# mLSTM sums over v from rounded halves, two gate rows through DRAM, and first outputs split behind the delta rule

## The chip, the cores and the metric

The kernel runs on one core of one Trainium2 chip. The metric is the device time of one execution, in microseconds (us). The core has five engines with an instruction queue each: TensorE (PE: matmuls and transposes, PEld: its weight loads), VectorE (DVE), ScalarE (ACT), GpSimd (POOL) and SyncE (SP, which here only issues DMAs). GpSimd computes little in this kernel; it issues the DMAs that are not of SP. All DMAs share 16 DMA engines.

## The reference

One layer of a hybrid encoder block in fp32, for 256 tokens of 2048 channels. The parts that matter here:

```
mod = silu(c) @ W_ada + b_ada     -> shift, scale, gate of the mixer; shift, scale, gate of the FFN
h   = RMSNorm(x) * (1 + scale_m) + shift_m
p   = h @ W_in                    -> inputs of the mLSTM (a), of the delta rule (b), merge gates
A   = bidirectional mLSTM         (4 heads, keys of 256, values of 512)
B   = bidirectional gated delta rule  (16 heads of 128)
y   = sigmoid(g_a) * (A @ W_a) + sigmoid(g_b) * (B @ W_b)
x   = x + gate_m * (y @ W_o)
x   = x + gate_f * SwiGLU(RMSNorm(x) * (1 + scale_f) + shift_f)      (width 5632)
```

and a last RMSNorm. For one head and one direction the mLSTM is a decayed attention, `h_t = sum_s P[t,s] v_s / max(|sum_s P[t,s]|, ...)`, where `P` is the product of query and key times the gates' decay.

## The kernel before

**Rounded halves.** The weights are fp32. The kernel splits each operand in two: a half `h` rounded to the format fp32r (a copy by ScalarE) and the remainder `l` (a subtraction by VectorE), and makes a product from three fp32r passes: `xh*wh`, `xl*wh`, `xh*wl`. `split(hi, lo, v)` does that for an operand that lies on the chip. `tjob` (L169) does it for a projection with two blocks of 128 tokens and 512 output columns: it loads the weights in chunks of 1.05 MB (`raw`, three buffers, issued on SP), splits each chunk as two halves of 128x1024 (`wh`, `wl`, three buffers each) and issues 12 passes of 512 columns for each half into two accumulators (`acc`). A chunk's `raw` buffer is free again when both its halves are split.

**Products that are not split.** A few products are made in plain fp32. Those of this change are the mLSTM's sums over `v` (`ph`, L977), whose operands are the decayed scores `dec` (tile `mdec`) and the values `vt`, and four products for each gate row.

**The order of the work.** The Python code is a set of generators that are advanced in turn (`fill`, `drive`, `steps`); a scheduler then orders each engine's instructions when the program is built, by priorities that follow that order and by its own estimates. `order(...)` keeps an instruction at its place in the order of the code. What comes out is a fixed order for each engine and each DMA queue: an instruction whose operand isn't there holds up all that stand behind it.

**The stretch around the change**, in the order of the code:

- The delta rule for its last four heads ends. Its outputs go through DRAM (`ob_d`) and come back as `o4_0` to `o4_3` (`o_load`, on GpSimd's queue). `o_split` makes of each a quarter of `obh` and `obl`, the operand of the projection `yb`.
- The loop of three: `fill(2)` issues the last products of the input projection (among them `ma3`, whose read-out is `ev_ma3` at L317), then `o_split(g)`.
- `y_b(g)`, g from 0 to 3, projects the delta rule's outputs with the weights `wbb`, four chunks for each g (`yb0_0` to `yb0_3`). Between its halves stand the steps of the four mLSTM heads, two at a time: `mlstm(h)` loads `mkq` (keys and queries), `vt`, `sgo` (the output gate) and `bc` (the decays) on GpSimd's queue; VectorE makes `mdec` by scans; TensorE makes the scores `psc`, then the denominators `pden`, then the sums `ph`; ScalarE reads out `dn` and `hs`. The result, normalised and times the gate, is transposed (`pxa`) into `hah` and `hal`.
- `y_a(g)` projects these with `wba`, merges both branches in `mg` and transposes that to `mgh` and `mgl`. Then comes the output projection `o0` to `o3`, whose `residual` reads `gm`, the mixer's gate as a row on all partitions.
- The FFN: gate and up projection (`gt`, `up`), down projection `d`, whose `residual` reads the other gate row, `gf`.

**The gate vectors.** `mod` holds the modulation with channels on partitions: 16 columns for each of its six parts. `ada_part` (L115) makes part 2 and the following ones in the background: for each column one load of 1.05 MB on SP (tile `ada`) and one multiply-and-sum on VectorE; `pump` advances them between the weight halves and `sums()` directly. `row(part, dst, ...)` (L1080) turns one part into a row on all partitions: for each quarter VectorE makes four scaled diagonals (`dg`), TensorE multiplies them by a matrix of ones, ScalarE copies the product to `dst`. It stands for `gm` behind the load of `x1`, ahead of the output projection, and for `gf` ahead of the down projection.

Of the kernel before, what the change touches and what calls it, by code (L numbers as in the profile page):

```python
# [9 lines left out]
F32 = mybir.dt.float32  # L10
# [5 lines left out]
P = 128  # L16
T = 256
D = 2048
# [34 lines left out]
def hybrid_block(ctx: ExitStack, tc: tile.TileContext, xr, nfr, crow, pk_d, cst_d, ada2, ada4, win0, winb, wint, wba, wbb, wo, wgu, wd, out, dbg=None):  # L53
# [31 lines left out]
    def order(ins, yes=True):  # L85

        return tc.keep_in_program_order(ins) if yes else ins
# [43 lines left out]

    background = []
# [36 lines left out]
    def tjob(name, chunks, xh, xl, done, early=0, by_token=None, steps=1):  # L169
# [6 lines left out]
        def halves(u, k0):  # L176
            if u not in raws:
                raws[u] = st.tile([P, 4, 512], F32, tag="raw", bufs=3, name=f"raw_{name}_{u}")
                nc.sync.dma_start(raws[u], chunks[u])
            wh = st.tile([P, 2, 512], F32R, tag="wh", bufs=3, name=f"wh_{name}_{u}_{k0}")  # L180
            wl = st.tile([P, 2, 512], F32R, tag="wl", bufs=3, name=f"wl_{name}_{u}_{k0}")
            order(S.activation(wh, raws[u][:, k0 : k0 + 2], AF.Copy), early)  # L182
            order(V.tensor_tensor(wl, raws[u][:, k0 : k0 + 2], wh.bitcast(F32), ALU.subtract), early)  # L183
            return wh, wl
# [45 lines left out]
    def run(job):  # L230
        for _ in job:
            pass
# [682 lines left out]
    def mlstm(h):  # L915
# [19 lines left out]
        for t in range(2):  # L935
# [17 lines left out]
            (0, 0): [(dec[:, 0, 0:P], 0)],  # L953
            (0, 1): [(dec[:, 0, P:256], 0), (dec[:, 0, 256:384], 1)],
            (1, 0): [(dec[:, 1, 256:384], 0), (dec[:, 1, 0:P], 1)],
            (1, 1): [(dec[:, 1, P:256], 1)],
        }
        pd_ = gps(f"pden{h}")
        for (d, t), terms in src.items():
            for i, (w, s) in enumerate(terms):  # L960
                PE.matmul(pd_[:, 2 * t + d : 2 * t + d + 1], w, ones1, start=i == 0, stop=i == len(terms) - 1)
# [8 lines left out]
        yield  # L970
        for t in range(2):
            pn = []
            for d in range(2):
                ph = gps(f"ph{h}_{t}_{d}")
                terms = src[d, t]
                for i, (w, s) in enumerate(terms):
                    PE.matmul(ph, w, vt[:, s], start=i == 0, stop=i == len(terms) - 1)  # L977
                pn.append(ph)
            S.activation(hs[:, t], pn[0], AF.Copy, scale=dn[:, t, 0:1])
            V.scalar_tensor_tensor(hs[:, t], pn[1], dn[:, t, 1:2], hs[:, t], ALU.mult, ALU.add)  # L980
            S.activation(sq, hs[:, t], AF.Square, accum_out=ss[:, t : t + 1])
            yield
# [19 lines left out]
    def y_b(g):  # L1002
# [6 lines left out]
        return tjob(f"yb{g}", [wbb[g, u] for u in range(4)], obh, obl, done)  # L1009
# [30 lines left out]
    for g in range(3):  # L1040
        fill(2)
        o_split(g, o4s[g])
# [10 lines left out]
    mg = mgp.tile([P, 2, D], F32, name="mg")  # L1053

# [8 lines left out]
    for g in range(4):  # L1063
        if g == 3:
            every[0] = 0
        run(y_a(g, mgh, mgl))
    while len(background) > 2:
        sums()
# [11 lines left out]
    def row(part, dst, rp, factor=1.0):  # L1080

        for g in range(4):
            dg = rp.tile([P, 4, P], F32, tag="dg", bufs=2, name=f"dg{part}_{g}")
            for e in range(4):
                c = part * KB + 4 * g + e
                V.tensor_scalar(dg[:, e], ident, mod[:, c : c + 1], factor, ALU.mult, ALU.mult)
            pr = gps(f"row{part}_{g}")
            PE.matmul(pr, ones, dg.rearrange("p e c -> p (e c)"), start=True, stop=True)
            S.activation(dst[:, g * 512 : (g + 1) * 512], pr, AF.Copy)

    gm = wp.tile([P, D], F32, name="gm")
    row(2, gm, wp, 0.5)
# [149 lines left out]
    row(5, gf, dp)  # L1242
# [134 lines left out]
```

## Time and profile before

| | us |
|---|---|
| timed, median of three | 1998.9 (1995.4 to 2001.5) |
| the profiled execution | 1998.51 |
| its span | 1996.5 |
| mean granted TensorE clock | 0.990 of full |

The span is the time from the first to the last instruction that the profile shows; the 2.0 us beside it lie around it. `L123` is line 123 of the kernel. A group is written `out<-in partitions x elements`, an engine's name ahead of the operation. `idle before` is the time that the engine stood still just ahead of those instructions, with the instruction or DMA that ended most of it.

### The profile page before, as it was taken

How to read it: one execution, taken by the hardware profiler on the slowest of the kernel's cores; microseconds unless marked ns; L12 is line 12 of the kernel's file. 1: busy time of each engine (PE TensorE's matmuls, PEld its weight loads, DVE VectorE, ACT ScalarE, POOL GpSimd, SP SyncE). 2: the span in 40 equal slices, each digit the busy share in tenths (PEclk: the TensorE clock that was granted, in tenths of full speed). 3: DMA queues.
4: the chain of work that ended last, by engine and by line, in shares of the span. 5: the costliest groups of instructions: out<-in, count | busy, mean ns of one | idle time of the engine just before them, and what ended most of it. 6: DMA issues, size and time to landing. Idle time of an engine off the chain costs nothing.

```text
span 1996.5 us, 26938 instructions
## 1 busy us (share of the span) xinstructions
PE 1935.0 (97%) x10310; PEld 1697.5 (85%) x10310; DVE 1392.7 (70%) x2099; ACT 1020.6 (51%) x1558; POOL 94.7 (5%) x181
## 2 busy tenths in 40 slices
PE   8998999999999889999899999899999999999997
PEld 6887889988989888989777888688888888888886
DVE  5777987778988787865677779765666665555554
ACT  3145757754774566555453444554444444444443
POOL 0001200110100010100100000000000000000000
PEclk9998999999999999999999999999999999999999
DMA  9986674567676665876787679457676675555553
GB/s 400 420 355 193 197 231 169 177 200 256 209 237 222 212 197 208 284 284 238 298 313 259 241 279 413 166 218 261 235 267 237 232 268 199 208 205 198 209 200 138
DMA packets 78322, 485.64 MB, mean 243 GB/s; under 512 B 10201, under 2 KB 15585, under 8 KB 23793
## 3 DMA queue, kind: packets, MB, share of 16 engines
q1 hardware_dynamic: 63360, 450.95, 62.2%
q0 software_dynamic: 7520, 17.88, 4.3%
q10 hardware_dynamic: 7314, 15.10, 2.0%
q8 instruction: 81, 1.33, 0.3%
q14 instruction: 47, 0.39, 0.1%
HBM read 467.07 MB, written 16.82 MB: 242 GB/s over the span
## 4 chain that ended last, share of the span: by engine, by line
PE 78%; DMA 9%; DVE 7%; ACT 4%; issue 2%; ACTq 0%; POOL 0%; SPq 0%; DVEq 0%; POOLq 0%
PE acc_up L200 4%; PE acc_up L203 4%; PE acc_up L201 4%; PE acc_d L203 4%; PE acc_d L201 4%; PE acc_d L200 4%; PE acc_gt L201 4%; PE acc_gt L200 4%; PE acc_gt L203 4%; DMA ra<-ada 3%; PE acc_b L161 3%; PE acc_o L203 2%; PE acc_o L200 2%; PE acc_o L201 2%; PE acc_a L161 2%; DMA raw_b<-winb 2%
## 5 line engine op out<-in xcount | busy, mean ns | idle before, releaser
L183 DVE TENSOR_TENSOR wl_d<-raw_d,wh_d 128x1024 fp32r<-128x1024 f32 x88 | 107.7, 1224 | 102.3 <-ACT wh_d L182 100.3
L183 DVE TENSOR_TENSOR wl_up<-raw_up,wh_up 128x1024 fp32r<-128x1024 f32 x88 | 107.7, 1225 | 101.2 <-ACT wh_up L182 101.2
L126 DVE SCALAR_TENSOR_TENSOR ada<-ada,crow 128x2048 f32<-128x2048 f32 x64 | 146.4, 2288 | 41.9 <-DMA ada<-ada 41.8
L182 ACT ACTIVATE wh_d<-raw_d 128x1024 fp32r<-128x1024 f32 x88 | 93.0, 1057 | 128.5 <-PE acc_d L201 122.8
L182 ACT ACTIVATE wh_gt<-raw_gt 128x1024 fp32r<-128x1024 f32 x88 | 92.9, 1056 | 120.7 <-PE acc_gt L201 73.2
L182 ACT ACTIVATE wh_up<-raw_up 128x1024 fp32r<-128x1024 f32 x88 | 93.0, 1057 | 120.5 <-PE acc_up L201 72.9
L183 DVE TENSOR_TENSOR wl_gt<-raw_gt,wh_gt 128x1024 fp32r<-128x1024 f32 x88 | 107.1, 1223 | 68.1 <-ACT wh_gt L182 47.3
L161 PE MATMUL acc_b<-hh,wh_b 128*128 128x256 f32 x576 | 140.8, 285 | 7.7 <-ACT wh_b L157 7.7
L161 PE MATMUL acc_b<-hl,wh_b 128*128 128x256 f32 x576 | 141.2, 286 | 0.0
L200 PE MATMUL acc_gt<-wh_gt,hfh 128*128 128x512 f32 x352 | 135.7, 385 | 0.1
L201 PE MATMUL acc_gt<-wh_gt,hfl 128*128 128x512 f32 x352 | 135.0, 384 | 0.0
L200 PE MATMUL acc_up<-wh_up,hfh 128*128 128x512 f32 x352 | 133.4, 379 | 0.0
L201 PE MATMUL acc_up<-wh_up,hfl 128*128 128x512 f32 x352 | 133.4, 379 | 0.0
L200 PE MATMUL acc_d<-wh_d,ffh 128*128 128x512 f32 x344 | 130.8, 380 | 0.0
L201 PE MATMUL acc_d<-wh_d,ffl 128*128 128x512 f32 x344 | 130.8, 380 | 0.0
L515 PE MATMUL first<-x,raw 128*128 128x256 f32 x512 | 114.5, 382 | 7.6 <-ACT x L508 7.6
L161 PEld LDWEIGHTS acc_b<-hh,wh_b 128*128 128x128 f32 x576 | 112.7, 196 | 9.9 <-ACT wh_b L157 8.3
L515 PEld LDWEIGHTS first<-x,raw 128*128 128x128 f32 x512 | 96.0, 190 | 26.1 <-ACT x L508 13.6
L161 PEld LDWEIGHTS acc_b<-hl,wh_b 128*128 128x128 f32 x576 | 112.9, 196 | 2.3 <-issue 2.2
L158 DVE TENSOR_TENSOR wl_b<-raw_b,wh_b 128x1024 fp32r<-128x1024 f32 x72 | 87.4, 1219 | 32.1 <-ACT wh_b L157 31.5
L157 ACT ACTIVATE wh_b<-raw_b 128x1024 fp32r<-128x1024 f32 x72 | 75.1, 1055 | 58.2 <-DMA raw_b<-winb 31.0
L182 ACT ACTIVATE wh_o<-raw_o 128x1024 fp32r<-128x1024 f32 x64 | 67.2, 1056 | 64.7 <-PE acc_o L201 27.2
(370 smaller groups left out, 4990.8 us busy)
## 6 DMA issues: line engine op xcount, KB each, us to landing
ada<-ada SPq DMA_DIRECT2D x64, 1024.0 KB, 5.2
raw_gt<-wgu SPq DMA_DIRECT2D x44, 1024.0 KB, 5.3
raw_up<-wgu SPq DMA_DIRECT2D x44, 1024.0 KB, 5.0
raw_d<-wd SPq DMA_DIRECT2D x44, 1024.0 KB, 4.9
raw_b<-winb SPq DMA_DIRECT2D x36, 1024.0 KB, 5.9
ra<-ada SPq DMA_DIRECT2D x32, 1025.0 KB, 15.7
raw<-win SPq DMA_DIRECT2D x16, 1024.0 KB, 14.5
raw_z<-wint SPq DMA_DIRECT2D x16, 1024.0 KB, 5.6
```

Of the source, the lines that this page charges most:

```text
L126: V.scalar_tensor_tensor(raw, raw, 1.0, row_c[:, :D], ALU.mult, ALU.mult, accum_out=mod[:, c0 + b : c0 + b + 1])
L157: S.activation(wh, raw[:, k0 : k0 + 8], AF.Copy)
L158: V.tensor_tensor(wl, raw[:, k0 : k0 + 8], wh.bitcast(F32), ALU.subtract)
L161: PE.matmul(o, wh[:, k], both(x, k0 + k).rearrange("p a b -> p b a"), start=k0 + k + i == 0, stop=False)
L182: order(S.activation(wh, raws[u][:, k0 : k0 + 2], AF.Copy), early)
L183: order(V.tensor_tensor(wl, raws[u][:, k0 : k0 + 2], wh.bitcast(F32), ALU.subtract), early)
L200: order(PE.matmul(ps[t], tok(xh, kk, t), turns(wh[:, k]), start=kk == 0, stop=False), early and steps > 1)
L201: PE.matmul(ps[t], tok(xl, kk, t), turns(wh[:, k]), start=False, stop=False)
L203: PE.matmul(ps[t], tok(xh, kk, t), turns(wl[:, k]), start=False, stop=kk == last)
L515: PE.matmul(first[o], raw[:, o], x[:, b], start=b == 0 and o % 2 == 0, stop=b == KB - 1 and o % 2 == 1)
```

## The change

There are three parts, which meet in the stretch described above.

1. *The sums over v* are made from rounded halves like the projections: `dec` is split to `dch` and `dcl`, `vt` to `vth` and `vtl`, and each of a head's six fp32 products becomes three fp32r passes. `vth` lies in the buffer of `o4_3`; the others lie in a new pool, `mp`. The generator stops once behind both blocks of tokens where it stopped behind each.
2. *The gate rows* are made by one transpose of the part's 16 columns (16 rows of 128), a copy on ScalarE, a store of the 2048 values to DRAM (`row_store`) and a load that puts them on all partitions (`row_load`), both on GpSimd's queue. For `gm` the store is called ahead of the last quarter of `ya`, and with it the loop over the leftover `sums()`; the load is called where `row` was. For `gf` both are called where `row` was.
3. *The outputs of the delta rule*: in the loop of three, `o_split(g)` is called ahead of `fill(2)`. And for the second chunk of `yb0` (halves 2 and 3, `held`) the two splits are kept at their place in the order of the code.

```diff
+    def row_store(part, rp, factor=1.0):
+        pr = gps(f"row{part}")
+        PE.transpose(pr[0:KB, 0:P], mod[:, part * KB : (part + 1) * KB], ident)
+        sm = rp.tile([KB, P], F32, name=f"rowsm{part}")
+        S.activation(sm, pr[0:KB, 0:P], AF.Copy, scale=factor)
+        G.dma_start(row_d[part].rearrange("(b p) -> b p", b=KB), sm)
+
+    def row_load(part, dst):
+        G.dma_start(dst, row_d[part].partition_broadcast(P))
...
-            order(S.activation(wh, raws[u][:, k0 : k0 + 2], AF.Copy), early)
-            order(V.tensor_tensor(wl, raws[u][:, k0 : k0 + 2], wh.bitcast(F32), ALU.subtract), early)
+            hold = early or 2 * u + k0 // 2 in held
+            order(S.activation(wh, raws[u][:, k0 : k0 + 2], AF.Copy), hold)
+            order(V.tensor_tensor(wl, raws[u][:, k0 : k0 + 2], wh.bitcast(F32), ALU.subtract), hold)
...
+        dch, dcl = (mp.tile([P, 2, 384], F32R, name=f"d{n}{h}", tag=f"d{n}", bufs=1) for n in ("ch", "cl"))
+        vth = ml.tile([P, 2, DV_A], F32R, tag="o4", bufs=1, name=f"vth{h}")
+        vtl = mp.tile([P, 2, DV_A], F32R, tag="vtl", bufs=1, name=f"vtl{h}")
+        split(dch, dcl, dec)
+        split(vth, vtl, vt)
         for t in range(2):
             pn = []
             for d in range(2):
                 ph = gps(f"ph{h}_{t}_{d}")
-                terms = src[d, t]
-                for i, (w, s) in enumerate(terms):
-                    PE.matmul(ph, w, vt[:, s], start=i == 0, stop=i == len(terms) - 1)
+                terms = [(x, y, *q) for x, y in ((dch, vth), (dcl, vth), (dch, vtl)) for q in src[d, t]]
+                for i, (x, y, c, s) in enumerate(terms):
+                    PE.matmul(ph, x[:, d, c : c + P], y[:, s], start=i == 0, stop=i == len(terms) - 1)
...
-            yield
+        yield
...
-        return tjob(f"yb{g}", [wbb[g, u] for u in range(4)], obh, obl, done)
+        return tjob(f"yb{g}", [wbb[g, u] for u in range(4)], obh, obl, done, held=() if g else (2, 3))
...
     for g in range(3):
+        o_split(g, o4s[g])
         fill(2)
-        o_split(g, o4s[g])
...
         if g == 3:
             every[0] = 0
+            while len(background) > 2:
+                sums()
+            row_store(2, ml, 0.5)
         run(y_a(g, mgh, mgl))
-    while len(background) > 2:
-        sums()
...
-    row(2, gm, wp, 0.5)
+    row_load(2, gm)
...
-    row(5, gf, dp)
+    row_store(5, dp)
+    row_load(5, gf)
```

How the built programs differ is seen at three places. The first is ScalarE's queue behind the delta rule. The first number behind a tile's name is its group, head or chunk (`wh_yb0_1_0` is the first half of `yb0`'s second chunk), the last only numbers the tile. Before:

```order
L182 ACTIVATE wh_yb0_0_2_9250<-raw_yb0_0_9232 128x1024
L182 ACTIVATE wh_yb0_1_0_9303<-raw_yb0_1_9301 128x1024
L317 ACT_TABLE_LOAD
L317 ACTIVATE ev_ma3_9208<-acc_ma3_0_9042 128x512
L317 ACTIVATE ev_ma3_9208<-acc_ma3_1_9043 128x512
L318 DMA ma_d3_109<-ev_ma3_9208 128x1024
L912 ACTIVATE obh_8828<-o4_0_8084 128x1024
L912 ACTIVATE obh_8828<-o4_1_8086 128x1024
L912 ACTIVATE obh_8828<-o4_2_8443 128x1024
```

And of the change, from the second quarter of `obh` on:

```order
L926 ACTIVATE obh_8830<-o4_1_8088 128x1024
L926 ACTIVATE obh_8830<-o4_2_8445 128x1024
L926 ACTIVATE obh_8830<-o4_3_8832 128x1024
L259 ACTIVATE vth0_9379<-vt0_8836 128x1024
L1004 ACTIVATE sgo0_8838<-sgo0_8838 128x1024
L259 ACTIVATE dch0_9377<-mdec0_9114 128x768
L1004 ACTIVATE sgo1_8847<-sgo1_8847 128x1024
L977 ACTIVATE dn0_9283<-pden0_9276 128x4
L998 ACTIVATE hs0_9288<-ph0_0_0_9385,dn0_9283 128x512
L977 ACTIVATE dn1_9298<-pden1_9291 128x4
L196 ACTIVATE wh_yb0_1_0_9308<-raw_yb0_1_9306 128x1024
```

The first split of `yb0`'s second chunk stood ahead of `ev_ma3` and of all of `obh`; it now stands behind all four quarters of `obh` and behind ScalarE's part of head 0 up to the first read-out of its sums.

The second place is TensorE's queue between the first and the third chunk of `yb0`. Before, where the scores of head 0 stood between two chunks:

```order
L203 MATMUL acc_yb0_0_9230<-wl_yb0_1_2_9320,obh_8828 128x512
L203 MATMUL acc_yb0_1_9231<-wl_yb0_1_2_9320,obh_8828 128x512
L203 MATMUL acc_yb0_0_9230<-wl_yb0_1_2_9320,obh_8828 128x512
L203 MATMUL acc_yb0_1_9231<-wl_yb0_1_2_9320,obh_8828 128x512
L937 MATMUL psc0_9117<-mkq0_8832 128x256 x4
L200 MATMUL acc_yb0_0_9230<-wh_yb0_2_0_9337,obh_8828 128x512
```

And of the change, behind the first chunk:

```order
L217 MATMUL acc_yb0_1_9236<-wl_yb0_0_2_9256,obh_8830 128x512
L951 MATMUL psc0_9119<-mkq0_8834 128x256 x4
L951 MATMUL psc1_9133<-mkq1_8843 128x256 x4
L975 MATMUL pden0_9276<-ones_81,mdec0_9114 128x1 x6
L975 MATMUL pden1_9291<-ones_81,mdec1_9128 128x1 x2
L996 MATMUL ph0_0_0_9385<-vth0_9379,dch0_9377 128x512
L996 MATMUL ph0_0_0_9385<-vth0_9379,dcl0_9378 128x512
L996 MATMUL ph0_0_0_9385<-vtl0_9380,dch0_9377 128x512
...
L996 MATMUL ph0_1_1_9406<-vtl0_9380,dch0_9377 128x512
L214 MATMUL acc_yb0_0_9235<-wh_yb0_1_0_9308,obh_8830 128x512
```

The scores of heads 0 and 1, denominators of both and all 18 passes of head 0's sums now stand between the first and the second chunk of `yb0`; before, the second chunk came first, only head 0's scores stood ahead of the third, and the rest came later.

The third place is the end of GpSimd's queue, behind the loads of heads 2 and 3. Before, nothing followed there:

```order
L924 DMA bc3_9761<-mal_d_93 128x256 x2
L919 DMA vt2_9748<-v_d2_100 128x1024
L919 DMA vt3_9757<-v_d3_101 128x1024
L921 DMA sgo2_9750<-o_d2_104 128x1024
L921 DMA sgo3_9759<-o_d3_105 128x1024
L1372 UNCONDITIONAL_BRANCH
```

And of the change:

```order
L935 DMA sgo2_9724<-o_d2_106 128x1024
L935 DMA sgo3_9733<-o_d3_107 128x1024
L140 DMA row_d2_89<-rowsm2_10663 16x128
L143 DMA gm_10837<-row_d2_89 128x2048
L140 DMA row_d5_90<-rowsm5_14920 16x128
L143 DMA gf_14915<-row_d5_90 128x2048
L1383 UNCONDITIONAL_BRANCH
```

Four DMAs are added there, a store and a load for each row.

More of the change, by code (lines that the diff above doesn't have):

```diff
@@ L129, in ada_part @@
         yield True
+    row_d = {part: tc.dram_tile([D], F32, name=f"row_d{part}") for part in (2, 5)}
+    def row_store(part, rp, factor=1.0):
[6 more added lines that the diff above has]
+        G.dma_start(dst, row_d[part].partition_broadcast(P))
     background = []
@@ L167, in fjob, with tjob @@
             yield True
-    def tjob(name, chunks, xh, xl, done, early=0, by_token=None, steps=1):
+    def tjob(name, chunks, xh, xl, done, early=0, by_token=None, steps=1, held=()):
         raws = {}
@@ L952, in mlstm @@
         src = {
[L953 to L956, printed above, removed]
+            (0, 0): [(0, 0)],
+            (0, 1): [(P, 0), (256, 1)],
+            (1, 0): [(256, 0), (0, 1)],
+            (1, 1): [(P, 1)],
         }
@@ L959, in mlstm @@
         for (d, t), terms in src.items():
-            for i, (w, s) in enumerate(terms):
-                PE.matmul(pd_[:, 2 * t + d : 2 * t + d + 1], w, ones1, start=i == 0, stop=i == len(terms) - 1)
+            for i, (c, s) in enumerate(terms):
+                PE.matmul(pd_[:, 2 * t + d : 2 * t + d + 1], dec[:, d, c : c + P], ones1, start=i == 0, stop=i == len(terms) - 1)
         dn = ml.tile([P, 2, 2], F32, tag="dn", bufs=2, name=f"dn{h}")
@@ L974, in mlstm @@
                 ph = gps(f"ph{h}_{t}_{d}")
-                terms = src[d, t]
-                for i, (w, s) in enumerate(terms):
-                    PE.matmul(ph, w, vt[:, s], start=i == 0, stop=i == len(terms) - 1)
+                terms = [(x, y, *q) for x, y in ((dch, vth), (dcl, vth), (dch, vtl)) for q in src[d, t]]
+                for i, (x, y, c, s) in enumerate(terms):
+                    PE.matmul(ph, x[:, d, c : c + P], y[:, s], start=i == 0, stop=i == len(terms) - 1)
                 pn.append(ph)
@@ L1053, in hybrid_block @@
     mg = mgp.tile([P, 2, D], F32, name="mg")
+    mp = pool(sd, "mp", side="right")
     every[0] = 2
@@ L1078, in hybrid_block @@
     S.dma_start(x1, xr)
[L1080 to L1089, printed above, removed]
     gm = wp.tile([P, D], F32, name="gm")
-    row(2, gm, wp, 0.5)
+    row_load(2, gm)
     def residual(t, g, ps, gate, ss, rp, hold=False):
```

## Prediction

> **What bounds the kernel now.** I read the page's busy times and chain first, then who TensorE waits for, then the stretch around the delta rule's end in five-microsecond windows, and last that stretch engine by engine in the timeline.
>
> ```profile
> span 1996.5 us, 26938 instructions
> PE 1935.0 (97%) x10310; PEld 1697.5 (85%) x10310; DVE 1392.7 (70%) x2099; ACT 1020.6 (51%) x1558; POOL 94.7 (5%) x181
> PE 78%; DMA 9%; DVE 7%; ACT 4%; issue 2%; ACTq 0%; POOL 0%; SPq 0%; DVEq 0%; POOLq 0%
> ```
>
> TensorE is busy for 97% of the span and is 78% of the chain. So a pass taken off TensorE is worth its length, and work put on VectorE or ScalarE is free as long as TensorE isn't made to wait for it. Who it waits for from the delta rule's end to the FFN:
>
> ```profile
> PE pxn L1184 <- ACT xn L1177: 8.4, 7, 3.4
> PE acc_yb L200 <- DMA ada<-ada: 6.0, 1, 6.0
> PE acc_o L203 <- DVE wl_o L183: 0.8, 2, 0.6
> ```
>
> The first row belongs to the norm ahead of the FFN, which the change leaves alone. The second is the place of this change: one wait of 6.0 us. In windows (PE busy, granted clock, DMA share, GB/s):
>
> ```profile
> 965.00:970.00 5.00, 4.07 (x19) 1.00 0.85 278
> 970.00:975.00 5.00, 0.00 (x0) 0.78 1.00 422
> 975.00:980.00 5.00, 4.86 (x11) 0.54 1.02 366
> ...
> 990.00:995.00 5.00, 5.00 (x25) 1.00 1.01 404
> 995.00:1000.00 5.00, 5.00 (x31) 1.00 1.04 386
> ```
>
> After the wait TensorE runs on half its clock for most of 975 to 980, which costs (1 - 0.54) x 5 = 2.3 us more; from 980 on it has no gap, while the DMA engines are full at 0.40 MB/us. ScalarE's, TensorE's and GpSimd's rows say why it waited:
>
> ```profile
> 969.91 1.06 ACT L182 ACTIVATE wh_yb<-raw_yb 128x1024 fp32r<-128x1024 f32 x1 [3.21 <-DMA raw_yb<-wbb]
> 970.98 1.28 ACT L317 ACT_TABLE_LOAD   x1
> 974.00 2.95 ACT L912 ACTIVATE obh<-o 128x1024 fp32r<-128x1024 f32 x3 [0.63 <-ACT ev_ma L317]
> ...
> 975.10 1.22 PE L200 MATMUL acc_yb<-wh_yb,obh 128*128 128x512 f32 x2 [6.04 <-DMA ada<-ada]
> ...
> 971.47 0.81 POOL L866 DMA_DIRECT2D o<-ob_d  x1 [123.51 <-ACT wh_yb L182]
> 985.12 0.54 POOL L924 DMA_DIRECT2D bc<-mal_d  x1 [0.73 <-DMA vt<-v_d]
> ```
>
> `obh`, which the first product of `yb0` reads, stood in ScalarE's line behind a split that waited for its weights. The mLSTM's loads for heads 0 and 1 go out on GpSimd's queue from 971.5 to 985.
>
> **The change, part by part.** *The sums over v.* A head had 6 fp32 products; it now has 18 of rounded halves.
>
> ```profile
> L977 PE MATMUL ph<-vt,mdec 128*128 128x512 f32 x48 | 22.0, 594 | 0.0
> 1192.03 0.86 PE row L1088 x2
> 1195.47 0.86 PE acc_o L203 x4
> ```
>
> 24 products are 48 passes, so an fp32 product is two; by the chain two such passes take 0.86 us and four passes of rounded halves the same 0.86, so 0.43 and 0.215 each. A head goes from 6 x 0.86 = 5.2 us to 18 x 0.215 = 3.9: **-1.3 us a head**, -3.9 for heads 1 to 3; head 0 is counted below with its surroundings. For each head the splits add an operation over 128x1024 and one over 128x768 to VectorE and to ScalarE:
>
> ```profile
> L183 DVE TENSOR_TENSOR wl_yb<-raw_yb,wh_yb 128x1024 fp32r<-128x1024 f32 x31 | 37.2, 1220 | 10.0 <-ACT wh_yb L182 9.9
> 980.00:1110.00 130.00, 129.88 (x591) 104.89 (x590) 98.35 (x142) 61.80 (x91) 7.39 (x13) 1.00 0.79 292
> ```
>
> On VectorE that is 4 x (1.22 + 0.92) = 8.6 us, the 768 columns scaled from 1024; ScalarE's two are shorter. VectorE is busy 98 of the 130 us of this stage (third figure) and ScalarE 62, so 107 of 130 still fits and I take nothing. Without that cover it would be those 8.6 us.
>
> *The gate rows.* Each row drops four fp32 products (4 x 0.86 = 3.45 us), 16 small VectorE products and four copies, and adds one transpose of 128 columns (0.22 us, a quarter of an 0.86), one copy and two DMAs on GpSimd. For `gf` nothing is near: its first reader is a whole group of the down projection later, 22 weight halves, some 57 us at the 2.59 us a half shown below. **-3.2 us.** `gm` loads 1.05 MB in the stage of the output projection:
>
> ```profile
> 1186.00:1250.00 64.00, 64.00 (x293) 54.35 (x292) 58.61 (x72) 29.30 (x37) 0.00 (x0) 1.00 1.01 416
> 1203.58 1.07 ACT L182 ACTIVATE wh_o<-raw_o 128x1024 fp32r<-128x1024 f32 x1 [1.44 <-DMA raw_o<-wo]
> 1208.25 0.38 PE L200 MATMUL acc_o<-wh_o,mgh 128*128 128x512 f32 x1
> ```
>
> The DMA engines have no room there for 64 us. The first weights of group 1 came in at 1203.6 and were split by 1204.65, 3.6 us before TensorE took them at 1208.25. With 1.05 / 0.416 = 2.5 us of transfer more ahead of them, TensorE can come at most 3.6 - 2.5 = 1.1 us earlier. Ends: -3.2 (the load slips in behind) and -1.1; by the row above I take **-1.1**. The Trainium skill's page "DMA: Bandwidth & Descriptors", section "Issuing engines are not separate DMA queues", says that transfers issued from different engines run on the same 16 DMA engines and interleave. By it GpSimd's queue buys this load no bandwidth, which is the -1.1; were the queue a path of its own, the sum would be 2.1 us lower. The trace's 1.01 agrees.
>
> The loop over the leftover sums moves ahead of the last quarter of `ya`. VectorE's order of sums is the same up to there, so it issues nothing at either place.
>
> *The place.* ScalarE's order now has all four `obh`, then `vth0`, `sgo0`, `dch0`, `sgo1`, `dn0`, `hs0`, `dn1`, and only then the second weights of `yb0`. `obh` no longer waits for weights, which saves the first 3 us of the old wait. But TensorE's order, too, has both heads' scores and all of head 0's sums between the first and second weights of `yb0`, where six halves of `yb0` ran before. Everything now stands behind head 0's chain, and that behind loads:
>
> ```profile
> 988.35 1.06 ACT L985 ACTIVATE sgo<-sgo 128x1024 f32<-128x1024 f32 x1 [2.56 <-DMA sgo<-o_d]
> 998.43 1.06 ACT L985 ACTIVATE sgo<-sgo 128x1024 f32<-128x1024 f32 x1 [3.15 <-DMA sgo<-o_d]
> ...
> 998.81 0.69 DVE L928 TENSOR_TENSOR_SCAN mdec<-bc,cst 128x256 f32<-128x256 f32 x1 [2.27 <-DMA bc<-mal_d]
> 1000.72 0.46 DVE L946 SCALAR_TENSOR_TENSOR mdec<-psc,eT,mdec 128x256 f32<-128x256 f32 x1
> ...
> 979.68 2.76 SPq L179 DMA_DIRECT2D raw_yb<-wbb  x2
> 987.08 0.33 SPq L125 DMA_DIRECT2D ada<-ada  x1
> ```
>
> The last load, head 1's `bc`, landed at 998.8, since three 1.05 MB loads of SP's ran beside GpSimd's in full DMA windows. Two of them (the second at 979.68 and the one at 987.08) need buffers that only the held splits set free, so they come later now: 2.1 / 0.40 = 5.2 us, and `bc` lands at **993.6**. Ends: 990.9 (all three out of the way, 7.9 us) and 998.8 (none). From there head 1's scans and first score product take 998.81 to 1001.18, so 2.4 us: TensorE gets its next row at 996.0. Then head 0's sums 3.9, six small rows 0.6 (half of the twelve below), and, as TensorE has idled again, the slow clock's 2.3 (ends 0 and 4.5): `yb0` goes on at **1002.8**. ScalarE's split for it is issued behind `dn1`, two thirds through the sums, and hides.
>
> Where was TensorE at 1002.8 before?
>
> ```profile
> 1000.55 0.38 PE L200 MATMUL acc_yb<-wh_yb,obh 128*128 128x512 f32 x1
> ...
> 1003.14 0.38 PE L200 MATMUL acc_yb<-wh_yb,obh 128*128 128x512 f32 x1
> ...
> 1003.79 1.40 PE L961 MATMUL pden<-ones,mdec 128*128 128x1 f32 x12
> 1005.04 3.68 PE L977 MATMUL ph<-vt,mdec 128*128 128x512 f32 x8
> ```
>
> A half of weights takes 2.59 us (1000.55 to 1003.14). At 1002.8 it had done five halves and 2.25 us of the sixth, 15.2 us, that are now still to do. In exchange head 0's sums (5.2) and head 1's twelve rows (1.25) are behind it now and were ahead then. So the place costs 15.2 - 5.2 - 1.25 = **+8.7 us**.
>
> The Trainium skill's page "TensorE: Matmul & The Clock Gate", section "Part 1: The HAM clock gate", has the clock at half after an idle window of about 3.4 us and whole again after a busy one. By it the long gap before 996 starts head 0's sums slow, as the 0.54 of 975 to 980 did; if only matmul-free time of that length mattered and the small rows kept the clock up, the place would cost 6.4.
>
> *Sum:* 8.7 - 3.9 - 3.2 - 1.1 = **+0.5 us**. The profiled execution took 1998.5 us, 2.0 of them outside its span, and the median is 1998.9; so about **1999**: no change.
>
> **Rivals.** *The loads come early.* `bc` lands at 990.9, the clock holds, and `gm` hides: -2.7 - 2.3 - 2.1 = -7.1, so **1992**. For it: SP has little to issue while the splits are held. Against: the DMA share of 1.01 in 970 to 1000, and the two loads before 979 still stand ahead of GpSimd's.
>
> *A second stall behind head 2's gate.* ScalarE's order has `sgo2` ahead of head 1's sums' read-out, `vth2` and the split of the second half of `yb1`; its load goes out only when head 0 is normalised.
>
> ```profile
> DMA to landing us min/median/max: 3.5/9.7/17.5
> ```
>
> That is the landing of the four `sgo` loads. Ten rows of ScalarE's and VectorE's between put the issue at about 1013.7; TensorE wants that half at 1002.8 + eight halves less one (18.1) + 3.9 = 1024.8, and ScalarE needs 4.7 us from the landing on. So the stall begins with a landing later than 6.4 us after the issue: nothing at 3.5, 3.3 us at the median, 11 at the longest. Half way between the last two it is **2006.5**, and slower. For it: VectorE's rows behind wait as well. Against: in the old order this load was one of the short ones, with GpSimd's queue nearly empty.
>
> *The row through DRAM gives nothing in the transfer-bound stage*: its 2.5 us come out of raw weights again further on, and the 1.1 is lost: **2000**, still no change.
>
> **How the numbers follow.** The forecast 0.5, loads early 0.2, second stall 0.17, row without gain 0.13. Within 0.3% of 1998.9, about what a measurement of this kernel can tell from no change, is 1992.9 to 2004.9: the first and the last, 0.63; faster 0.2; slower 0.17. The range takes in the ends of the landing (-2.7, +5.2), the clock (-2.3, +2.2), `gm` (-2.1) and the middle of the second stall: 1990 to 2007.
>
> **What would show it.** The wait of 6.0 us at `acc_yb` splits: a short one before the first weights, and waits of 10 to 16 us in all for `mkq`, `mdec` or `bc` before the sums; `bc` lands near 993.6; `yb0`'s second weights start near 1002.8, with a granted clock under 0.7 just before. 72 `ph` passes near 0.215; no `dg` rows; `wh_o` waits longer for `raw_o`. The forecast is wrong if TensorE shows less than 8 us of new idle time there, or a wait of over 2 us on `wh_yb` or `wl_yb` later in the stage.

## The result

The changed kernel takes 2000.4 us (median of 20 runs) beside 1994.7 us of the kernel before (20 runs): ratio 1.0028, with a 95% interval from 1.0017 to 1.0038. It is 5.7 us slower, just inside the 0.3% that the forecast called no change; the forecast was 0.5 us slower. (The forecast's 1999 stood on three runs of the kernel before with a median of 1998.9; over twenty it is 1994.7. So the 0.5 is what to compare, not the 1999.) The page of its profile has the same shape as before: a span of 1999.4 us, with TensorE busy for 1934.1 of it (97%).

**Where the time went.** I cut both profiled executions at the same pieces of work: the ends of the last products of `ma`, `ya`, `o`, `up` and `d`. So the first row is the stretch with `yb`, the mLSTM and `ya`, the second the output projection, the third the norm with gate and up projection, the fourth the down projection. Columns: start and end, length, busy time of PE, PEld, DVE, ACT and POOL, granted clock, DMA share, GB/s. The kernel before:

```profile
969.07:1183.38 214.31, 208.11 (x953) 172.78 (x954) 155.09 (x200) 101.03 (x131) 12.37 (x21) 0.98 0.77 281
1183.38:1272.13 88.75, 87.94 (x401) 74.34 (x399) 80.25 (x96) 39.77 (x53) 0.00 (x0) 1.00 0.91 366
1272.13:1754.05 481.92, 473.44 (x2225) 412.69 (x2226) 288.00 (x282) 225.72 (x257) 0.00 (x0) 0.99 0.64 227
1754.05:1986.28 232.23, 232.23 (x1072) 201.56 (x1071) 122.44 (x127) 99.83 (x109) 0.00 (x0) 1.00 0.55 190
```

And the changed kernel:

```profile
964.99:1191.33 226.34, 213.94 (x978) 183.77 (x979) 163.17 (x208) 105.79 (x139) 12.86 (x22) 0.95 0.74 266
1191.33:1279.21 87.88, 84.83 (x392) 72.79 (x391) 77.48 (x80) 37.05 (x49) 0.55 (x1) 1.00 0.93 382
1279.21:1760.30 481.09, 472.96 (x2225) 413.12 (x2226) 287.88 (x282) 225.38 (x257) 0.00 (x0) 0.99 0.63 228
1760.30:1989.21 228.91, 228.91 (x1066) 200.31 (x1064) 119.43 (x111) 97.65 (x106) 1.05 (x2) 1.00 0.57 197
```

The first stretch is 12.0 us longer. The three others are shorter by 0.9, 0.8 and 3.3. That is +7.0 in all, near the timed 5.7. The profiled execution of the changed kernel happened to reach the end of `ma` 4.1 us sooner (964.99 against 969.07), in work that the change leaves alone; over all runs below, that point lies between 964.99 and 970.49. So stretches are compared from here on, not clock times.

In the first row TensorE's idle time (length less busy time) grew from 6.20 to 12.40, by 6.2 us. Its busy time grew too, by 5.8, although the sums over v take less. Who it waits for in the place of the old wait of 6.0 us:

```profile
PE psc L951 <- DMA mkq<-kq_d: 7.7, 2, 6.4
PE acc_yb L214 <- ACT obh L926: 2.6, 1, 2.6
```

The wait ahead of `yb0` is shorter, as forecast. The new one is for the keys and queries of the mLSTM's heads. Then the clock around that wait (same columns as above), and TensorE's rows. In each of the eleven traces the clock changes only at whole multiples of 3.41 us from one change to the next, so each row is one window of that length; the first row takes three in one. A window at 0.50 is called slow from here on.

```profile
975.10:985.33 10.23, 3.82 (x17) 2.73 (x15) 3.78 (x4) 3.07 (x3) 2.07 (x4) 1.00 1.02 388
985.33:988.74 3.41, 2.10 (x5) 1.74 (x6) 2.65 (x8) 0.83 (x2) 1.90 (x4) 0.50 1.03 390
988.74:992.16 3.42, 3.42 (x14) 3.06 (x14) 3.27 (x7) 1.17 (x2) 0.96 (x2) 0.50 0.80 294
992.16:995.57 3.41, 3.41 (x13) 3.12 (x14) 1.19 (x6) 0.59 (x2) 0.86 (x2) 0.50 0.83 233
995.57:998.98 3.41, 3.41 (x12) 2.83 (x12) 0.75 (x1) 0.27 (x1) 0.00 (x0) 0.50 0.01 2
998.98:1002.40 3.42, 3.42 (x9) 2.74 (x10) 2.45 (x5) 3.19 (x5) 0.00 (x0) 0.50 0.00 0
1002.40:1005.81 3.41, 3.41 (x17) 2.95 (x17) 3.41 (x5) 3.41 (x6) 0.00 (x0) 1.00 0.60 163
```

```profile
986.64 3.78 PE L951 MATMUL psc<-mkq 128*128 128x256 f32 x8 [6.41 <-DMA mkq<-kq_d]
990.22 3.41 PE L975 MATMUL pden<-ones,mdec 128*128 128x1 f32 x16
993.49 0.77 PE L996 MATMUL ph<-vth,dch 128*128 128x512 f32 x1
...
994.92 0.42 PE L975 MATMUL pden<-ones,mdec 128*128 128x1 f32 x2
...
997.90 1.27 PE L975 MATMUL pden<-ones,mdec 128*128 128x1 f32 x6
...
1002.75 0.38 PE L214 MATMUL acc_yb<-wh_yb,obh 128*128 128x512 f32 x1
```

The clock is at half for five windows, 17.1 us, in four of which TensorE never stops. Head 0's sums take 9.3 us (993.49 to 1002.75) in place of 3.9 and the small rows among them. In what it does there, one thing stands out: the `pden` rows, products of one column.

### The profile page after: what moved, and what is told of

Same layout as the page of the kernel before. It is cut to its first block, busy times and chain, and to the rows that moved or that the text cites. A ratio compares the mean times of both kernels' runs of the same rounds, so it can differ in the third digit from the quotient of the medians.

```text
span 1999.4 us, 26949 instructions
## 1 busy us (share of the span) xinstructions
PE 1934.1 (97%) x10320; PEld 1706.4 (85%) x10320; DVE 1394.9 (70%) x2075; ACT 1021.6 (51%) x1560; POOL 96.8 (5%) x185
## 4 chain that ended last, share of the span: by engine, by line
PE 75%; DMA 10%; DVE 7%; issue 4%; ACT 4%; POOL 0%; ACTq 0%; SPq 0%; DVEq 0%; POOLq 0%
PE acc_up L214 4%; PE acc_up L217 4%; PE acc_up L215 4%; PE acc_d L215 4%; PE acc_d L217 4%; PE acc_d L214 4%; PE acc_gt L215 4%; PE acc_gt L214 4%; PE acc_gt L217 4%; PE acc_b L174 3%; DMA ra<-ada 2%; PE acc_a L174 2%; PE acc_o L217 2%; PE acc_o L214 2%; PE acc_o L215 2%
```

## The experiments

The theories that the expectations speak of: **A**, the whole loss comes from the held splits of `yb0`'s second chunk, and the other parts gain what was forecast; **B**, the place costs only the forecast 8.7 us, and the splits and the DMAs eat the rest; **C**, the half clock is the cost in the place; **D**, it is the chain of loads and steps, whatever the clock; **E**, the one-column denominators keep the clock at half; **F**, the waits alone do.

Each run was timed beside the kernel before anew, so the ratio is what to compare.

| run | ratio to before (95%) | median, us | first stretch, us | TensorE busy in it |
|---|---|---|---|---|
| before | 1 | 1994.7 to 1997.0 | 214.31 | 208.11 |
| changed | 1.0028 (1.0017 to 1.0038) | 2000.4 | 226.34 | 213.94 |
| no_held | 0.9964 (0.9944 to 0.9985) | 1988.1 | 212.56 | 205.52 |
| held_only | 1.0096 (1.0070 to 1.0123) | 2013.6 | 231.63 | 218.34 |
| warm_clock | 1.0019 (0.9999 to 1.0039) | 1999.3 | 222.23 | 213.37 |
| chunk_first | 0.9981 (0.9962 to 1.0001) | 1992.0 | 213.67 | 206.61 |
| rows_only | 0.9981 (0.9963 to 1.0000) | 1993.5 | 214.77 | 208.67 |
| wide_den_held | 1.0004 (0.9989 to 1.0019) | 1996.5 | 219.71 | 207.99 |
| wide_den_free | 0.9965 (0.9946 to 0.9984) | 1988.2 | 211.12 | 204.51 |
| chunk_then_keys | 0.9984 (0.9967 to 1.0002) | 1995.0 | 219.26 | 208.04 |
| third_between | 0.9975 (0.9958 to 0.9991) | 1991.1 | 212.50 | 206.44 |

The timings carry 2 to 5 us of uncertainty each, so the small steps are read from the stretches.

### no_held: without the held splits

```diff
-        return tjob(f"yb{g}", ..., obh, obl, done, held=() if g else (2, 3))
+        return tjob(f"yb{g}", ..., obh, obl, done)
```

> The changed kernel without the two splits kept in program order (held); the built order is that of before at the place, with the sums over v from halves and both gate rows through DRAM still in. Theory A (the held second chunk carries the whole loss, the other parts gain what the forecast gave them, four heads by 1.3, 3.2 and 0.9 us): 9.3 us under the kernel before, some 1985.4 beside its 1994.7, ratio 0.9953; the wait at the first weights of yb0 is back at about 6 us. Theory B (the splits and the DMAs on GpSimd's queue cost about what they save, and the place costs only the forecast 8.7 us): within 2 us of the kernel before, and about 4 to 8 us under the changed kernel.

7.1 us faster than before, 0.9964. The built order without `held` is, row for row on all engines, the one that also has `o_split` at its old place: the early call of `o_split` moves nothing by itself, `held` moves everything. The stretches against before: -1.7, -0.2, -0.8 and -3.3, -6.1 in all. A holds and B falls, but the first stretch gains only 1.7 us of the 5.2 that A gave the sums; a slow window that this execution has and the kernel before has not (under wide_den_free, below) took part of the rest. The wait at `yb0`'s first weights is back, as A has it:

```profile
PE acc_yb L214 <- DMA ada<-ada: 6.1, 1, 6.1
```

### held_only: the held splits alone

```diff
     for g in range(3):
+        o_split(g, o4s[g])
         fill(2)
-        o_split(g, o4s[g])
...
+        return tjob(f"yb{g}", ..., obh, obl, done, held=() if g else (2, 3))
```

The base is the kernel before: sums over v in fp32, rows by diagonals.

> The kernel before with the third part alone: the outputs split ahead of the fills and the splits of the second chunk of yb0 held; sums in fp32, rows by diagonals. Theory A: the held chunk costs what the change costs in all plus what its other parts save, 5.7 + 9.3 = 15 us, ratio 1.0075; TensorE shows some 10 us of waits between the first and the second chunk of yb0 and over 15 us at half clock there. Theory B: 4 to 8.7 us, ratio 1.002 to 1.0045.

18.5 us slower, 1.0096. The other stretches are those of before to 0.02 us; the first has 17.3 us more (231.63). Busy time is 10.2 us over before's with the same work to do: that is slow clock. Idle time is 13.29, 7.1 us over before's. A holds with a somewhat larger price than the 15 it named, of which about a us is a slow window further on that is chance (1097.12, under wide_den_free); B's 4 to 8.7 is out. Between the first and the second chunk there are 7.8 us of waits for keys, where A had some 10, and five slow windows, 17.1 us, where it had over 15.

### rows_only: the gate rows alone

The base is the kernel before, with the change's second part (`row_store`, `row_load`, and the leftover sums called ahead of the last quarter of `ya`).

> The kernel before with both gate rows through DRAM and nothing else of the change. Forecast: the row of the down projection 3.2 us, that of the output projection 1.1, so 4.3 us under the kernel before, ratio 0.9978; the stretch from the end of the output projection to the end of the down projection 3.2 us shorter than before's 714.15, the output projection's 88.75 by 1.1. Rival (the row's load only moves the wait to the next weights): the output projection as long as before, the sum 3.2 us.

```profile
1179.97:1268.27 88.30, 84.83 (x393) 72.74 (x391) 77.47 (x80) 37.16 (x49) 0.55 (x1) 1.00 0.93 380
...
1748.49:1977.40 228.91, 228.91 (x1066) 200.16 (x1064) 119.42 (x111) 97.67 (x106) 1.05 (x2) 1.00 0.57 197
```

The down projection is 3.3 us shorter, and TensorE is busy throughout: the forecast's 3.2. In the output projection TensorE has 3.1 us less to do (87.94 to 84.83), but the stage gains only 0.45 here and 0.87 in the changed kernel: the rest comes back as waits for weights, in the changed kernel 2.5 us:

```profile
PE acc_o L214 <- ACT wh_o L196: 2.5, 2, 2.0
```

So the rival's nothing is nearer to this run's 0.45 than the forecast's 1.1, and the other kernels say the same: with the row through DRAM this stage takes 87.88 to 88.76 us in six of them and 89.01 to 89.27 in the three that have a slow window in it, beside 88.75 with the diagonals. The gain is 0 to 0.9 us, 0.2 in the middle of the six.

From the end of the output projection to the end of the down projection the run is 5.0 us shorter (709.13 beside 714.15), where 3.2 was expected. The other 1.7 lies in the gate and up projections, which the edit leaves alone. Part of it is clock: of the nine kernels with the rows through DRAM, that stage takes 480.2 to 480.4 us in the three with one slow window in it and 480.8 to 481.1 in the six with two or three; before it takes 481.9, with two. The moved sums cost at most half a us (first stretch 214.77 beside 214.31).

### warm_clock: TensorE kept busy through the wait

```diff
         psc = gps(f"psc{h}")
+        for _ in range(9 if h == 1 else 0):
+            PE.matmul(psc[:, 0:384], ident, cst[:, 0:384], start=True, stop=True)
```

> The changed kernel with nine needless fp32 products of 384 columns ahead of head 1's scores (their results are overwritten), which fill TensorE's wait for head 1's keys with about 5.8 us of passes and end before those keys land. If the half clock behind that wait is the cost (theory C), the 17 us at half clock are gone, the sums start no earlier than VectorE gives head 1's decays (about 992) but run at 3.9 us in place of 9, and yb0 goes on about 5 us sooner: 4 to 6 us under the changed kernel. If the chain's order and loads set the time and not the clock (theory D), no difference, or up to 3 us more where the needless passes end too late.

The stretch is 4.1 us shorter than the changed kernel's (222.23 against 226.34). The time, 1.0019, can't be told from the changed kernel's: in the profiled execution a slow window in the output projection (89.27 us) and an end of `ma` that came 3.55 us later went the other way. It also has a slow window behind heads 2 and 3 that the changed kernel has not (under wide_den_free). The clock behind the wait:

```profile
985.77:1002.00 16.23, 14.82 (x70) 11.10 (x70) 10.88 (x26) 5.82 (x9) 4.17 (x7) 1.00 0.78 270
```

So C holds: with the clock whole, the sums end sooner, at 1001.89, 33.4 us behind `ma`'s end, where the changed kernel has 37.8. D holds for their start: they begin 28.2 us behind `ma`'s end (996.77 less 968.54) and 28.5 in the changed kernel (993.49 less 964.99), since VectorE's decays of head 1 come first.

```profile
996.30 0.61 PE L977 MATMUL pden<-ones,mdec 128*128 128x1 f32 x4 [1.41 <-DVE mdec L962]
996.77 0.48 PE L998 MATMUL ph<-vth,dch 128*128 128x512 f32 x1
```

### wide_den_held: denominators of 128 columns

```diff
-                PE.matmul(pd_[:, 2 * t + d : 2 * t + d + 1], dec[:, d, c : c + P], ones1, ...)
+                PE.matmul(pd_[:, (2 * t + d) * P : (2 * t + d + 1) * P], dec[:, d, c : c + P], ones, ...)
-        S.activation(dn, pd_[:, 0:4].rearrange("p (t d) -> p t d", t=2), AF.Abs)
+        S.activation(dn, pd_.rearrange("p (t d w) -> p t d w", t=2, d=2)[:, :, :, 0], AF.Abs)
```

> The changed kernel with the denominators' products 128 columns wide in place of one (all columns hold the same sum, one is read). Theory E (rows of one column count as nearly no work for the clock, so that head 1's denominators among head 0's sums hold the clock at half): the windows in which they stand are busy now, the clock is back by about 992 in place of 1002.4, head 0's sums take about 5 us in place of 9.3, and the stretch from the end of ma to the end of ya falls from 226.3 by some 4 us, less up to 1 us for the wider rows. Theory F (the clock stays down for the waits alone, whatever the denominators are): half clock as long as in the changed kernel, the stretch 226 to 228 us.

The first stretch falls by 6.6 us to 219.71, and the time to 1.0004: making the denominators 128 times as wide made the kernel faster. Behind the wait for head 1's keys the clock is at half for two windows in place of five:

```profile
986.32:989.73 3.41, 1.76 (x4) 1.49 (x5) 2.98 (x8) 0.87 (x2) 1.97 (x4) 0.50 1.02 386
989.73:993.15 3.42, 3.42 (x13) 2.95 (x13) 2.95 (x6) 1.50 (x2) 1.05 (x2) 0.50 0.87 319
993.15:996.56 3.41, 3.41 (x25) 3.16 (x25) 1.84 (x10) 1.53 (x4) 1.07 (x2) 1.00 0.82 234
```

The middle window is the one to compare with the changed kernel's from 988.74 to 992.16: in both TensorE is busy from end to end with the last scores and the first denominators, at half clock. Behind the one-column rows the next window is slow again; behind the wide ones the clock is whole. E holds here; F, which wanted 226 us or more, falls. The scheduler moved denominators and sums of head 1 as well, so not all of the 6.6 is the clock's: up to the second chunk of `yb0`, which starts 32.9 us behind `ma`'s end (999.09) in place of 37.8, the gain is 4.8, and 1.8 comes further on.

### wide_den_free: the same without the held splits

Both edits, that of no_held and that of wide_den_held.

> The changed kernel without held, and with the denominators 128 columns wide. In the kernel without held one window of 3.41 us at half clock stood right behind the 24 one-column products of heads 2 and 3, with no wait ahead of it. Theory E: that window is gone, and the stretch from ma's end to ya's end is 1 to 2 us under its 212.6. Theory F: the window comes and goes by chance, and the stretch is 212.6 or longer by the wider rows, at most 1 us.

The stretch is 1.4 us under no_held's, as E had it. By chance the two executions line up to a few hundredths at heads 2 and 3. TensorE's rows of their denominators, in no_held and then wide:

```profile
1060.52 0.28 PE L975 MATMUL pden<-ones,mdec 128*128 128x1 f32 x2
...
1061.61 2.53 PE L975 MATMUL pden<-ones,mdec 128*128 128x1 f32 x22
1064.00 0.78 PE L214 MATMUL acc_yb<-wh_yb,obh 128*128 128x512 f32 x1
```

```profile
1060.50 0.61 PE L975 MATMUL pden<-ones,mdec 128*128 128x128 f32 x4
...
1061.81 2.39 PE L975 MATMUL pden<-ones,mdec 128*128 128x128 f32 x20
1063.96 0.46 PE L214 MATMUL acc_yb<-wh_yb,obh 128*128 128x512 f32 x1
```

The wide ones take no longer: 2.39 us for 22 and 2.15 for 20, 0.11 each, start to start. The windows around them, no_held's first:

```profile
1060.56:1063.97 3.41, 3.41 (x29) 3.30 (x28) 1.98 (x2) 1.23 (x2) 0.00 (x0) 1.00 0.82 345
1063.97:1067.38 3.41, 3.41 (x10) 2.78 (x10) 3.28 (x3) 0.17 (x1) 0.00 (x0) 0.50 0.92 386
```

```profile
1058.81:1062.22 3.41, 3.41 (x21) 3.09 (x20) 2.98 (x4) 1.48 (x2) 0.00 (x0) 1.00 0.79 279
1062.22:1065.64 3.42, 3.42 (x26) 3.23 (x26) 2.35 (x3) 0.35 (x2) 0.00 (x0) 1.00 0.93 386
1065.64:1069.05 3.41, 3.41 (x18) 2.98 (x17) 2.71 (x8) 1.55 (x2) 0.00 (x0) 1.00 0.82 264
```

In no_held TensorE is busy without a gap, and behind a window that holds 2.5 us of one-column products the next one is slow. With wide products no window is slow. But this pair changes two things at once. The beat of 3.41 us on which the clock changes lies elsewhere in each execution: in no_held one window takes in all but one of the 24 rows, while in wide_den_free the clock falls at 970.07 and is back at 976.90, and steps of 3.41 us from there cut the rows in two, 7 and 17. What the beat alone does, two kernels with one-column products show, each with its 24 rows in one piece. First held_only, where they lie in one window:

```profile
1094.47 2.73 PE L975 MATMUL pden<-ones,mdec 128*128 128x1 f32 x24
1093.71:1097.12 3.41, 3.41 (x29) 3.30 (x28) 2.01 (x2) 1.23 (x2) 0.00 (x0) 1.00 0.80 259
1097.12:1100.54 3.42, 3.42 (x9) 2.75 (x9) 2.13 (x1) 0.17 (x1) 0.00 (x0) 0.50 0.85 352
```

Then rows_only, where a window's end falls among them:

```profile
1073.89 2.73 PE L975 MATMUL pden<-ones,mdec 128*128 128x1 f32 x24
1071.99:1075.40 3.41, 3.41 (x25) 3.17 (x23) 2.06 (x2) 1.13 (x2) 0.00 (x0) 1.00 0.76 245
1075.40:1078.82 3.42, 3.42 (x22) 3.15 (x23) 2.15 (x1) 0.59 (x3) 0.00 (x0) 1.00 0.88 369
1078.82:1082.23 3.41, 3.41 (x17) 2.80 (x16) 3.34 (x11) 1.79 (x2) 0.00 (x0) 1.00 0.61 190
```

Of the eight kernels with one-column products, the three whose execution has 22 or more of these rows in one window (no_held, held_only, warm_clock) have a slow window behind it, and the five whose beat cuts them in two, 10 to 14 in a window, have none. So E is right that a window full of such rows counts as idle, and F is right that here the slow window comes and goes by chance. Whether the width or the beat kept the clock whole in wide_den_free this run doesn't tell; it is wide_den_held that shows the width at work. The timed ratios, 0.9964 and 0.9965, show no difference.

TensorE's busy time is 1.0 us lower without that slow window (205.52 to 204.51), and the sums' own saving is plain against rows_only, which has none at heads 2 and 3 either: 208.67 to 204.51, 4.2 us for four heads.

### Three orders meant to be better

All three keep `held`. chunk_first calls for the second chunk ahead of the mLSTM's steps:

```diff
     fill(2)
     o_split(3, o4s[3])
+    fill(2)
     for gen in (cores, steps(mlstm(2), mlstm(3))):
```

> The changed kernel with the two halves of yb0's second chunk called for ahead of the mLSTM's first steps, still held: ScalarE's order has all four quarters of obh, then the second chunk's splits, then head 0's steps, and TensorE's has the second and third chunk between the two heads' scores. Theory A: the place now gains, as obh waits for no weights (3 us of the old wait of 6.0) and no chain stands ahead of the second chunk; 9.3 + about 3 = 12 us under the kernel before, ratio 0.994. Rival: TensorE waits at head 0's scores, which stand ahead of the second chunk, for keys that land up to 8 us after the first chunk's start, and the gain over the kernel without held is nothing or negative.

213.67 us, 1.1 more than no_held. The rival was right:

```profile
PE acc_yb L214 <- ACT obh L926: 2.6, 1, 2.6
...
PE acc_ya L214 <- ACT hah L1017: 2.0, 1, 2.0
PE psc L951 <- DMA mkq<-kq_d: 1.9, 1, 1.9
```

The wait for `obh` is 2.6 us, but head 0's scores wait 1.9 for their keys ahead of the second chunk, and `ya` waits 2.0 for the last heads.

chunk_then_keys also moves the scores behind that chunk and keeps TensorE's products of both in this order:

```diff
-    fill(4)
-    next(cores)
...
     o_split(3, o4s[3])
+    fill(2)
+    next(cores)
...
-                order(PE.matmul(ps[t], ...), early and steps > 1)
+                order(PE.matmul(ps[t], ...), early and steps > 1 or n in held)
...
-                PE.matmul(psc[:, t * T : (t + 1) * T], ...)
+                order(PE.matmul(psc[:, t * T : (t + 1) * T], ...))
```

> The changed kernel with the second chunk of yb0 still held, but called for ahead of the mLSTM's scores, which are called for behind it, and with TensorE's first products of that chunk and the scores kept in this order: TensorE's order has the first and second chunk, then head 0's scores. Theory A: the wait at yb0's first weights is 2.7 us in place of 6.0, no wait for keys stands ahead of the second chunk, and the stretch from ma's end to ya's end falls 3 us under the 212.6 of the kernel without held, to about 209.5; 10 us under the kernel before, ratio 0.995. Rival: the transposes of heads 2 and 3 wait at the end of the stretch as in the run with the second chunk first (2.0 and 0.5 us), and half of it is lost.

A miss: 219.26 us. The second chunk now waits itself, since its splits stand on ScalarE behind the last quarter of `obh`, and that quarter's load, issued at 967.75, lands at 977.3 with the DMA engines full (a share of 1.00 from 968.55 to 977.60):

```profile
PE acc_yb L214 <- ACT wh_yb L196: 3.2, 1, 3.2
```

```profile
977.34 1.06 ACT L926 ACTIVATE obh<-o 128x1024 fp32r<-128x1024 f32 x1 [7.28 <-DMA o<-ob_d]
```

TensorE's idle time in the stretch is 11.2 us (219.26 less 208.04): these 3.2, 2.9 for `obh`, 2.5 for `hah` and 0.5 at the transposes of the last heads, which the rival had at 2.0 and 0.5, 1.2 for `wl_yb`, and two short ones. Its busy time is 2.5 us over no_held's, which was not followed. The timed ratio, 0.9984, is better than this one profile.

third_between splits the third quarter of `obh` between the two chunks, so that the held splits stand ahead of the fourth, and has the wide denominators:

```diff
-        o_split(g, o4s[g])
+        if g < 2:
+            o_split(g, o4s[g])
         fill(2)
...
+    fills[:] = [y_bs()]
+    fill(2)
+    o_split(2, o4s[2])
     so.close()
```

> The changed kernel with wide denominators and with the third quarter of obh split between the first and the second chunk of yb0, so that the held splits of the second chunk stand behind the third quarter and ahead of the fourth, whose load lands last, and ahead of head 0's steps; TensorE's order is that of the kernel without held. Theory A: the wait at yb0's first weights is 2.7 us as in the changed kernel in place of 5.9, the second chunk's weights are there when the first is through (no wait over 1 us for them or for keys), and the stretch from ma's end to ya's end is 2 to 3 us under the 211.1 of the kernel without held and with wide denominators: 208 to 209, some 10 us under the kernel before, ratio 0.995. Rival (the second chunk's load or head 0's keys land too late for the earlier start, so the 3 us come back as waits further on): 211 or more.

212.50 us, 1.4 more than wide_den_free; the rival again. The wait ahead of `yb0` is 2.8 in place of 5.9, but waits of 0.6 for `obl`, 0.7 at the scores and 1.4 at `hah` come back, so that idle time falls by 0.55 only (6.06 beside 6.61). Busy time is 1.9 us longer. More work meets the two slow windows behind the wait (6.26 us of them in place of 5.42); most of the 1.9 was not followed.

The best versions are the two without `held`: 0.9964 and, with wide denominators, 0.9965. Both beat the kernel before and the changed one.

## Why the prediction was near, and which step of it failed

The number was near in part by luck. By the stretches the change costs 7.0 us where the forecast had 0.5; the timed 5.7 lies just inside the 6.0 that the forecast called no change, and 0.8 us in the gate and up projections, for which the forecast has no term, helped. One of the forecast's own signs of being wrong came: under 8 us of new idle time. TensorE waits 7.7 us for keys (6.2 more idle time in all), where 10 to 16 were forecast; the rest of the cost is slow clock.

- **The gate rows**: `gf` was right, 3.2 forecast and 3.3 measured. `gm` was forecast at 1.1 and measured at 0.9 in the changed kernel, but at 0 to 0.45 in the five others that have no slow window in this stage. The reason was right (3.1 us of TensorE's work gone, most of it back as waits for weights); the size was nearer to the rival of a row that gives nothing in this stage, and the 0.9 is at the lucky end.
- **The moved sums and the splits on VectorE and ScalarE** cost at most half a us (first stretch of rows_only 214.77 beside 214.31 for the moved sums; idle time of wide_den_free 6.61 beside rows_only's 6.10 for the splits), where the forecast had nothing.
- **The sums over v** were a little too cheap: 1.3 us a head forecast, 1.05 measured (4.2 for four). The 0.215 us of a pass in a long row of products held less well in these short ones; 18 passes in a row (one head's, in the changed kernel) take 4.1 us where the forecast had 3.9:

```profile
1089.12 0.40 PE L996 MATMUL ph<-vth,dch 128*128 128x512 f32 x1
...
1093.22 0.38 PE L214 MATMUL acc_yb<-wh_yb,obh 128*128 128x512 f32 x1
```

- **The place**: the mechanism was right, the term was mis-sized. `yb0`'s second weights started at 1002.75 where the forecast had 1002.8, but that is chance: `ma` ended 4.1 us sooner in this execution. Counted from `ma`'s end the resume came at 37.8 us and not at 33.7. The decays' load was right: head 1's `bc` landed at 990.0 (its second half, issued at 980.76, took 9.2 us), 25.0 us behind `ma`'s end, where the forecast had 24.5. TensorE waited for the keys of that head and not for `bc`.
- **The step that failed** is "as TensorE has idled again, the slow clock's 2.3 (ends 0 and 4.5)". The price was taken from the stretch behind the old wait, where full products followed and the clock came back within two windows. Here scores and one-column denominators followed, some of them among the sums, and the clock stayed at half for five. With the clock whole behind the wait (warm_clock) the resume comes at 33.4 us in place of 37.8, so the slow clock cost at least 4.4, nearly twice the term; the rest of the chain was at most 1.9 us longer than the forecast's 31.4 (33.7 less the 2.3). Wide denominators, which leave two windows slow, bring the resume to 32.9.
- **What is left**: the first stretch cost 12.0 where the place less heads 1 to 3 was forecast at 8.7 - 3.9 = 4.8, 7.2 too little. Of that 4.0 stand at the resume, 0.8 in the sums of three heads (3.1 saved in place of 3.9) and 1.4 in idle time behind the resume (1.5 us beside 0.1 before, most of it waits for the heads' transposes); 1.0 was not followed.
- **The rivals**: the loads did not come early; the second stall behind `sgo2` did not come (that load landed 4.6 us after its issue, under the 6.4 that the rival needed; ScalarE waited 0.75 us for it, at 1016.60, and TensorE for no weights of `yb` there for over 0.3 us). The outcome lies between the forecast and that rival by size, with neither's reason: the clock's 2.1 over its term are just within the +2.2 that the range allowed, and the longer chain, the sums and the later waits came on top.

What stays open: the 0.8 us by which the gate and up projections are shorter in the changed kernel than before, with two slow windows in both, and why the short rows of the sums take 0.228 us a pass.

## What to carry to other kernels

Pinning one instruction on an in-order engine puts everything behind it behind the loads ahead of it: list what now stands ahead of the next long stretch of matmuls, and when its loads land, before moving it. Price a wait on TensorE by what follows it too: the old wait was priced at 2.3 us of slow clock ahead of full products, and the new one cost 4.4 ahead of narrow ones. Widen narrow products that stand behind a wait, where the width is free as here. Compare the clocks of two executions on each one's own beat, since rows at the same time need not lie in the same window. And compare executions by stretches between the same pieces of work: here the down projection takes 228.90 or 228.91 us in each of the nine kernels that have its row through DRAM, while whole runs of one kernel scatter over 14 us (1987.4 to 2001.5).

## What the runs showed of the hardware

The granted clock does not follow the profile's busy time of TensorE. In no_held a window in which TensorE was busy for 3.41 of 3.41 us, 2.5 of them with weight loads and products of one column, was followed by a window at 0.50, and so it was in held_only and warm_clock. In the five executions whose beat cut the same 24 rows in two, 10 to 14 in a window, the clock stayed whole: what counts is how much of one window the narrow rows fill, and the beat lies elsewhere in each execution. At half clock, busy windows with such rows (988.74 to 998.98 in the changed kernel) did not bring the clock back, not even the last, with a third of them; the first one full of 512-column products (998.98 to 1002.40) did, and so did one with scores and 128-column denominators (989.73 to 993.15 in wide_den_held).

The Trainium skill's page "TensorE: Matmul & The Clock Gate", section "Part 1: The HAM clock gate", says that the clock falls after an idle window of some 3.4 us and returns after a busy one. The length agrees with the windows of 3.41 us here; its "idle" has to be read to take in rows of narrow products, which the profile counts as busy. And a weight load with a 128-column fp32 product behind it costs no more than one with a single column (0.11 us start to start for both), so the width that brought the clock back in wide_den_held was free.
